# A hybrid decoder trunk: the written order kept on three engines during the channel MLPs, and the mixer's steps spread over each of them

## The chip, the cores and the metric

The kernel runs on one core of a Trainium2 chip. The metric is the device time of one execution in microseconds (us). Three runs of the kernel before took 2379.74, 2380.16 and 2384.47 us; their median, 2380.16 us, is the time to compare with. In what follows PE is TensorE, DVE is VectorE, ACT is ScalarE and SP is the engine whose queue issues the transfers; PEld rows are PE's weight loads.

## The reference, cut to what matters

Two layers over 1024 tokens of width 1024, in fp32:

```python
for i in range(DEPTH):                       # DEPTH = 2
    z = rmsnorm(h) @ w_in                    # 1024 -> 1280
    ya = chunk_gmlp(z_a)                     # gated MLP over chunks of 128 tokens
    yb = swa_sink_attention(z_q, z_k, z_v)   # 8 heads, window of 128 tokens, a sink per head
    yc = s5_ssm(z_c)                         # 16 groups of a complex recurrence, and a GLU
    h = h + concat(norm(ya), norm(yb), norm(yc)) @ w_out
    h = h + square(relu(norm(h) @ w_ff1)) @ w_ff2              # 1024 -> 4096 -> 1024
    h = h + sigmoid(norm(h) @ w_ple_gate) * (p[i] @ w_ple_proj)
```

The first four lines of the loop are called the mixer here, the last two the channel MLP and the gate.

## The kernel before

The tokens are cut into two halves of 512 columns. Every product is made of three matmuls in a split format (high x high, low x high, high x low), each 128 x 128 weights against 512 columns. So each weight tile is cast once on ACT (`load_w`, L104: the high part) and once on DVE (L105: the low part), and waits in a ring of three for the MLP (`ringf`) and of two for the mixer (`ringm`).

After a prelude (about 0 to 385 us: the mixer of layer 0 for half 0, projections of both halves) come four **windows**, one for each layer and half: (0,0), (0,1), (1,0), (1,1). In a window, `window()` writes eight chunks of the channel MLP and then eight gate tiles. A chunk has an up part, four tiles of 24 matmuls, each read by DVE (`r`, L1344), squared twice on ACT (`A`, `q`, L1346 and L1347) and split by DVE (L1348); and a down part, eight tiles of 12 matmuls, each added to `H` by DVE (L1333). In the last chunk each of these also feeds the sum of squares `nacc` and the next `x`. From `nacc` a matmul and a chain that changes between DVE and ACT (`rstd_wide`) make the scale `rbc`. A gate tile is 24 matmuls, then `gt` on DVE (L1390), a tanh on ACT (L1391), two operations on DVE (L1392, L1394, which finishes `H`), and in layer 1 four transposes on PE (`po`, L1400), a copy on ACT and the store. In layer 0 the window instead ends with `rstd_lane`, which makes the next layer's scale (`rv`, `dg`) and spreads it with a matmul.

While a window is written, the mixer of the half that comes next is written too, as a **lane**: a generator that yields after each step. After every 12 matmuls of the window `main` calls `tick`, and each lane advances by its rate:

```python
    def tick(self):
        for e in list(self.lanes):
            e[2] += e[1]
            while e[2] >= 1.0 and not e[3]:
                e[2] -= 1.0
                self.step(e)
```

In attention one step makes the scores `pss` of a unit (four heads of a block of 128 queries) and its softmax (`anm`, `pr`, `aden` on DVE, four exponentials on ACT), another its transposes `pt` and the product `po`, another the transposed queries `pq`.

None of this fixes the order on the engines. The code runs under a scheduler that sees the whole program, and places the instructions of each engine by its own forecast of when their inputs are ready; the order written serves as priority. Each engine then runs its list from front to end, as the rows of the trace do.

Of the kernel before, what the change touches and what calls it, by code (L numbers as in the profile page):

```python
# [38 lines left out]
PASSES = ((0, 0), (1, 0), (0, 1))  # L39


RATE, RATE0, RATEL = 3.0, 2.0, 3.0


class Ring:
# [11 lines left out]
    def next(self):  # L57
        while len(self.loaded) <= self.ahead and self.load():
            pass
        return self.loaded.pop(0)  # L60


class Trunk:
# [1033 lines left out]
    def k_steps(self, c):  # L1097


        V, S, T, at, nb, k = self.V, self.S, self.T, c["at"], c["nb"], c["k"]  # L1100
        fl = lambda x: x.rearrange("p h b a -> p (h b) a")
        f = fl(self.hf)[:, c["b0"]:c["b0"] + nb, 8:10]
        V.tensor_tensor(k, k, f.unsqueeze(3).to_broadcast([P, nb, 2, 64]), ALU.mult)
        t2 = at.tile([P, nb, 2, 64], F32, tag="rt2", name="kt2")
        tc, ts = c["tab"][1][:, 0], c["tab"][1][:, 1]
        for s in range(2):
            V.tensor_tensor(t2[:, :, :, s * 32:s * 32 + 32], k[:, :, :, 32 - s * 32:64 - s * 32],
                            ts[:, :, s].unsqueeze(2).to_broadcast([P, nb, 2, 32]), ALU.mult)
        V.tensor_tensor(k, k, tc.rearrange("p b a d -> p b (a d)").unsqueeze(2).to_broadcast([P, nb, 2, 64]), ALU.mult)
        V.tensor_tensor(k, k, t2, ALU.add)  # L1110
        c["kT"] = at.tile([P, 2, 2, nb, P], F32R, name="kT")
        yield
        for i in range(nb):
            kst = at.tile([P, 2, 3, 64], F32R, tag="kst", name="kst")
            S.copy(kst[:, :, 0], k[:, i])
            S.copy(kst[:, :, 2], k[:, i])
            V.tensor_tensor(kst[:, :, 1], k[:, i], kst.bitcast(F32)[:, :, 0], ALU.subtract)
            pk = self.ps.tile([P, 512], F32, tag="t", name="pk")
            for j in range(4):
                T.matmul(pk[:, j * P:(j + 1) * P], kst[:, j // 2, j % 2:j % 2 + 2].rearrange("p a d -> p (a d)"),  # L1120
                         self.identr, start=True, stop=True)
            S.copy(c["kT"][:, :, :, i], pk.rearrange("p (g s c) -> p g s c", g=2, s=2))
            yield
# [31 lines left out]
    def attn_steps(self, c, ql):  # L1155

        h = c["h"]
        units = [(4 * h + b, gk) for b in range(4) for gk in range(2)]
        n, st, late = len(units), {}, []
        for p in range(-1, n + 3):  # L1160
            if 0 <= p - 2 < n:
                blk, gk = units[p - 2]
                self.attn_pv(c, blk, gk, st.pop(p - 2))
                if gk == 1:
                    yield from self.wait(("z", c["l"], h))
                    self.attn_sum(c, blk)
                    if blk % 2:
                        late.append((p, blk - 1, self.attn_rstd(c)))
            if 0 <= p - 1 < n:
                self.attn_pt(c, *units[p - 1], st[p - 1])  # L1170
            yield
            if late and late[0][0] < p:
                self.attn_out(c, *late.pop(0)[1:])
            if 0 <= p < n:
                st[p] = self.attn_softmax(c, *units[p], self.attn_scores(c, *units[p], st[p]))
            yield
            if p + 1 < n:
                blk, gk = units[p + 1]
                st[p + 1] = self.attn_q(c, blk, gk)
                if gk:  # L1180
                    next(ql, None)
            yield

    def attn_q(self, c, blk, gk):
        qst = c["qst"][blk]
        pq = self.ps.tile([P, 512], F32, tag="t", name="pq")
        for i in range(4):
            self.T.matmul(pq[:, i * P:(i + 1) * P], qst[:, gk * 4 + i].rearrange("p a d -> p (a d)"), self.identr,
                          start=True, stop=True)
        qt = c["at"].tile([P, 4, P], F32R, name="qt")  # L1190
        self.S.copy(qt.rearrange("p a b -> p (a b)"), pq)
        return qt
# [286 lines left out]
    def run(self):  # L1479
        self.setup()  # L1480
        zws, self.zw = ExitStack(), None
        self.zw = self.pool(zws, "zw", 4, side=self.side(0), reuse_waits="tile")
        xs, xp = self.stage("xin", 0)
        left = self.lane(self.left_lane(), RATEL)
        for _ in self.first_x(0, xp, left):
            pass
        x1 = self.lane(self.first_x(1, xp))
        gen = self.project0()
        z0 = self.lane(gen)
        self.until(lambda: x1[3] and ("zq", 0, 0) in self.flags)  # L1490
        xs.close()
        self.until(lambda: {"zg", "rotary"} <= self.flags)
        zws.close()
        self.lanes.remove(z0)
        pzs = ExitStack()
        self.zpools.append(self.pool(pzs, "pz", 2, side=self.side(0), reuse_waits="tile"))
        self.lane(self.gmlp(0, 0, 0, "x", [("attn", 0, 0)]), RATE0)
        self.until(lambda: True)
        self.lane(self.attention(0, 0, 0), RATE0)
        self.main(gen)  # L1500
        self.main(self.embed())
        self.until(lambda: {("attn", 0, 0), ("gm", 0, 0)} <= self.flags)
        self.zpools.pop()
        pzs.close()
        self.finish(self.lane(self.mix_out(0, 0, self.fring, "mm", 3)))
        seq = [(l, h) for l in range(DEPTH) for h in range(2)]
        nxt = left
        for i, (l, h) in enumerate(seq):
            self.window(l, h, self.stages(*seq[i + 1]) if i + 1 < len(seq) else set())
            if i + 1 < len(seq):  # L1510
                self.finish(nxt)
            if i + 2 < len(seq):
                nxt = self.lane(self.mix_lane(*seq[i + 2]), RATE)


def build(tc, a):
# [27 lines left out]
```

## Time and profile before

| | |
|---|---|
| median of three runs | 2380.16 us |
| the profiled execution, its own time | 2385.95 us |
| its span, first to last instruction | 2384.2 us |
| PE busy, share of the span | 98% |
| PE weight loads busy | 79% |
| DVE busy | 65% |
| ACT busy | 43% |
| mean granted TensorE clock | 0.990 |
| chain that ended last: PE's share | 83% |

The profile is of one execution; 1.75 us of its time lie outside the span. Ends of matmuls are modelled, so PE counts as busy a little beyond the moment at which it could issue the next one. A row of the timeline gives the start, the duration and, in brackets, how long the engine was idle before it and what released it.

### The profile page before, as it was taken

What the parts mean: (1) busy time and instruction counts of PE and PEld (TensorE: products, weight loads), DVE (VectorE), ACT (ScalarE), POOL (GpSimd) and SP (SyncE); (2) the same over time, 40 slices, a digit from 0 to 9 for tenths busy, and PEclk for the clock granted to TensorE, in tenths of its full rate; (3) what the DMA queues carried; (4) which work ended last, traced back from release to release, by engine and by line L of the source; (5) the groups of instructions that cost most, each with busy time, mean ns of one, the idle gap of its engine ahead of it and who ended that gap; (6) DMA issues with size and microseconds to landing.
All of it is one profiled execution on the core that took longest, in us unless ns stands there. A gap on an engine that the chain in (4) does not pass through costs nothing.

```text
span 2384.2 us, 29265 instructions
## 1 busy us (share of the span) xinstructions
PE 2325.3 (98%) x10941; PEld 1885.4 (79%) x10941; DVE 1552.8 (65%) x2700; ACT 1027.8 (43%) x1787; POOL 5.4 (0%) x15
## 2 busy tenths in 40 slices
PE   7998899999999999999999999999999999999998
PEld 5886687788788887777888888777888887888887
DVE  7877767675966765676585774676657674444455
ACT  7427646433334443553342543464334343322333
POOL 0000000000000000000000000000000000000000
PEclk9998999999999999999999999999999999999999
DMA  8663632253553335324443344522534334333333
GB/s 244 188 203 119 208 99 64 80 173 106 145 156 102 111 125 155 95 78 140 123 135 124 98 145 124 145 72 76 166 105 135 124 97 134 97 96 94 94 97 98
DMA packets 403558, 295.94 MB, mean 124 GB/s; under 512 B 66668, under 2 KB 376024, under 8 KB 401624
## 3 DMA queue, kind: packets, MB, share of 16 engines
q1 hardware_dynamic: 403416, 294.07, 41.1%
q8 instruction: 86, 1.41, 0.3%
q14 instruction: 56, 0.46, 0.1%
HBM read 250.48 MB, written 43.54 MB: 123 GB/s over the span
## 4 chain that ended last, share of the span: by engine, by line
PE 83%; DMA 7%; DVE 5%; ACT 3%; issue 2%; SPq 1%; ACTq 0%; DVEq 0%
PE mm_ps L359 43%; PE x_ps L359 20%; PE s_ps L359 8%; DMA st<-in_w_in 2%; DVE w L105 2%; PE s_ps L710 1%; PE po L1259 1%; PE pss L1201 1%; ACT w L104 1%; PE p_ps L359 1%; DMA st<-in_w_out 1%; PE p_ps L947 1%; DMA yu<-ye 1%; PE pt L1238 1%; SPq L98 1%
## 5 line engine op out<-in xcount | busy, mean ns | idle before, releaser
L104 ACT CAST w<-st 128x1024 fp32r<-128x1024 f32 x364 | 387.9, 1067 | 853.1 <-PE mm_ps L359 430.0
L359 PE MATMUL mm_ps<-x,w 128*128 128x512 f32 x2904 | 708.4, 396 | 7.9 <-ACT x L89 4.2
L359 PEld LDWEIGHTS mm_ps<-x,w 128*128 128x128 f32 x2904 | 544.5, 190 | 133.0 <-issue 10.1
L105 DVE TENSOR_TENSOR w<-st,w 128x1024 fp32r<-128x1024 f32 x364 | 448.5, 1234 | 202.6 <-ACT w L104 191.6
L359 PE MATMUL mm_ps<-A,w 128*128 128x512 f32 x2016 | 500.8, 392 | 2.5 <-DVE H L1333 2.5
L359 PEld LDWEIGHTS mm_ps<-A,w 128*128 128x128 f32 x2016 | 375.7, 188 | 85.4 <-DVE H L1333 4.9
L359 PE MATMUL x_ps<-A,w 128*128 128x512 f32 x1056 | 272.8, 393 | 4.1 <-DVE H L1333 4.1
L359 PE MATMUL x_ps<-x,w 128*128 128x512 f32 x1104 | 272.2, 394 | 0.0
L359 PE MATMUL s_ps<-x,w 128*128 128x512 f32 x1056 | 252.4, 391 | 4.8 <-DVE w L105 2.6
L359 PEld LDWEIGHTS x_ps<-x,w 128*128 128x128 f32 x1104 | 205.6, 188 | 45.6 <-issue 3.4
L359 PEld LDWEIGHTS s_ps<-x,w 128*128 128x128 f32 x1056 | 198.1, 188 | 49.1 <-DVE w L105 4.0
L359 PEld LDWEIGHTS x_ps<-A,w 128*128 128x128 f32 x1056 | 196.5, 188 | 51.0 <-DVE H L1333 8.3
L1333 DVE TENSOR_TENSOR H<-H,mm_ps 128x512 f32<-128x512 f32 x168 | 113.2, 683 | 84.2 <-PE mm_ps L359 83.3
L1344 DVE SCALAR_TENSOR_TENSOR r<-mm_ps,rbc 128x512 f32<-128x512 f32 x88 | 60.7, 690 | 119.2 <-PE mm_ps L359 119.2
L710 PE MATMUL s_ps<-w,x 128*128 128x512 f32 x384 | 101.3, 404 | 4.1 <-ACT x L89 2.6
L1333 DVE TENSOR_TENSOR H<-H,x_ps 128x512 f32<-128x512 f32 x88 | 60.2, 684 | 68.8 <-PE x_ps L359 68.2
L1348 DVE TENSOR_TENSOR A<-q,A 128x512 fp32r<-128x512 f32 x128 | 87.8, 686 | 6.8 <-ACT q L1347 6.6
L710 PEld LDWEIGHTS s_ps<-w,x 128*128 128x128 f32 x384 | 73.6, 194 | 20.8 <-ACT x L89 3.0
L1346 ACT ACTIVATE A<-r 128x512 fp32r<-128x512 f32 x128 | 80.2, 627 | 8.1 <-DVE r L1344 7.9
L1347 ACT ACTIVATE q<-r 128x512 f32<-128x512 f32 x128 | 78.9, 617 | 0.0
L1224 ACT ACTIVATE pr<-pr,anm,hf 128x128 f32<-128x128 f32 x128 | 61.6, 485 | 17.4 <-DVE anm L1221 17.4
L89 ACT ACTIVATE x<-H,gT 128x512 fp32r<-128x512 f32 x80 | 53.7, 711 | 13.5 <-PE s_ps L359 7.7
(386 smaller groups left out, 2112.3 us busy)
## 6 DMA issues: line engine op xcount, KB each, us to landing
st<-in_w_ff SPq DMA_DIRECT2D x256, 512.0 KB, 4.1
st<-in_w_out SPq DMA_DIRECT2D x32, 512.0 KB, 4.1
st<-in_w_ple_gate SPq DMA_DIRECT2D x32, 512.0 KB, 4.1
st<-in_w_in SPq DMA_DIRECT2D x18, 512.0 KB, 4.4
p<-par SPq DMA_DIRECT2D x8, 1024.0 KB, 8.5
pj<-pjz SPq DMA_DIRECT2D x32, 256.0 KB, 2.2
H<-hs SPq DMA_DIRECT2D x4, 2048.0 KB, 7.9
pj<-pj SPq DMA_DIRECT2D x32, 256.0 KB, 3.4
```

The costliest lines, as they stand in the source:

```text
L89: self.S.activation(hi, x, AF.Copy, scale=g)
L98: self.Q.dma_start(sv[:, :, c0:c1], src)
L104: self.S.copy(hi, src)
L105: self.V.tensor_tensor(lo, src, hi.bitcast(F32), ALU.subtract)
L359: self.T.matmul(ps, w[:, i, k, c0:c0 + P], X[:, j, k, :], start=(start and n == 0), stop=(stop and n == last))
L710: T.matmul(pss[b], X[:, j, 2 * s + kk, c], w[:, i, kk, :], start=(s == 0 and kk == 0 and n == 0), stop=(s == 3 and kk == 1 and n == 2))
L1224: S.activation(pr[:, i], pr[:, i], AF.Exp, bias=nm[:, i:i + 1], scale=f[:, i:i + 1], accum_out=den[:, i:i + 1])
L1333: V.tensor_tensor(H[:, m], H[:, m], ps, ALU.add)
L1344: V.scalar_tensor_tensor(r, ps, 0.0, self.R[h][1], ALU.max, ALU.mult)
L1346: S.activation(A[:, 0, m], r, AF.Square)
L1347: S.activation(q, r, AF.Square)
L1348: V.tensor_tensor(A[:, 1, m], q, A.bitcast(F32)[:, 0, m], ALU.subtract)
```

## The change

Three things change. All four windows are written inside `manual_schedule` for PE, DVE and ACT: on these three engines the instructions of that part keep the order in which the code writes them. SP's and POOL's order stays the scheduler's. The rate of a mixer lane falls from 3.0 steps a tick to 1.15, and that of the lane that runs on into the first window to 1.25. And two yields are added, one in `k_steps` and one in each round of `attn_steps`, except in the prelude's attention: a round is four steps long where it was three.

```diff
-RATE, RATE0, RATEL = 3.0, 2.0, 3.0
+RATE, RATEW, RATE0, RATEL = 1.15, 1.25, 2.0, 3.0
+ENGINES = {mybir.EngineType.PE, mybir.EngineType.DVE, mybir.EngineType.Activation}
@@ k_steps
         c["kT"] = at.tile([P, 2, 2, nb, P], F32R, name="kT")
         yield
+        if c["l"] or c["h"]:
+            yield
@@ attn_steps
             yield
+            if c["l"] or h:
+                yield
@@ run
         nxt = left
-        for i, (l, h) in enumerate(seq):
-            self.window(l, h, self.stages(*seq[i + 1]) if i + 1 < len(seq) else set())
-            if i + 1 < len(seq):
-                self.finish(nxt)
-            if i + 2 < len(seq):
-                nxt = self.lane(self.mix_lane(*seq[i + 2]), RATE)
+        nxt[1] = RATEW
+        with self.tc.manual_schedule(engines=ENGINES):
+            for i, (l, h) in enumerate(seq):
+                self.window(l, h, self.stages(*seq[i + 1]) if i + 1 < len(seq) else set())
+                if i + 1 < len(seq):
+                    self.finish(nxt)
+                if i + 2 < len(seq):
+                    nxt = self.lane(self.mix_lane(*seq[i + 2]), RATE)
```

The work is the same. What moves is the order on each engine, at three places above all. (The lines of the change stand 4 to 11 lower than those of before: L359 becomes L363, L1400 becomes L1408.)

First, PE at the very end, in the gate tiles of the last window. `s_ps`, `p_ps`, `x_ps` and `mm_ps` are the gate tiles, `po` the transposes of a finished `H`. Before:

```order
L359 MATMUL mm_ps<-x_18296,w 128x512 x24
L359 MATMUL s_ps<-x_18296,w 128x512 x24
L359 MATMUL p_ps<-x_18296,w 128x512 x24
L359 MATMUL mm_ps<-x_18296,w 128x512 x4
L1400 MATMUL po<-identr,H_13998 128x128 x4
L359 MATMUL mm_ps<-x_18296,w 128x512 x20
L359 MATMUL s_ps<-x_18296,w 128x512 x2
L1400 MATMUL po<-identr,H_13998 128x128 x4
```

And now, from the last rows of the down part on:

```order
L292 MATMUL o_ps<-nacc,onesr 128x512
L363 MATMUL s_ps<-x_18298,w 128x512 x24
L1408 MATMUL po<-identr,H_15295 128x128 x4
L363 MATMUL x_ps<-x_18298,w 128x512 x24
L1408 MATMUL po<-identr,H_15295 128x128 x4
L363 MATMUL mm_ps<-x_18298,w 128x512 x24
L1408 MATMUL po<-identr,H_15295 128x128 x4
```

The first transposes stood behind five gate tiles and four matmuls of the sixth; now those of each tile stand directly behind its own 24 matmuls.

Second, PE at the end of the first window, where the next layer's scale is made (`o_ps<-onesr,nacc` sums the squares, `o_ps<-dg,onesr` spreads the scale; `w,x_7513` and `w,x_7515` are the next mixer's projection). Before:

```order
L359 MATMUL mm_ps<-x_5521,w 128x512 x9
L273 MATMUL o_ps<-onesr,nacc 128x1 x4
L359 MATMUL mm_ps<-x_5521,w 128x512 x15
L359 MATMUL x_ps<-x_5521,w 128x512 x20
L317 MATMUL o_ps<-dg,onesr 128x512
L359 MATMUL x_ps<-x_5521,w 128x512 x4
```

Now:

```order
L363 MATMUL s_ps<-x_6990,w 128x512 x24
L363 MATMUL x_ps<-x_6990,w 128x512 x24
L277 MATMUL o_ps<-onesr,nacc 128x1 x4
L321 MATMUL o_ps<-dg,onesr 128x512 x2
L363 MATMUL mm_ps<-x_6627,w 128x512 x12
L714 MATMUL s_ps<-w,x_7515 128x512 x12
```

The 35 matmuls of the next window that stood between the two, and the 9 and more before the first, now follow both.

Third, DVE in the attention of the first window. Before, one softmax in the down part of a chunk:

```order
L1214 COPY_PREDICATED pr<-pmask,pss 128x256 x2
L1219 TENSOR_REDUCE anm<-pr 128x4
L1220 TENSOR_TENSOR anm<-anm,nhf 128x4
L1221 TENSOR_TENSOR anm<-anm,nsk 128x4
L1227 TENSOR_TENSOR aes<-anm,sinks 128x4
L1333 TENSOR_TENSOR H_3113<-H_3113,x_ps 128x512
L1333 TENSOR_TENSOR H_3113<-H_3113,mm_ps 128x512 x2
L1229 TENSOR_TENSOR aden<-aden,aes 128x4
L1230 RECIPROCAL aden<-aden 128x4
L1231 TENSOR_TENSOR pr<-pr,aden 128x512
```

Now, one in the up part:

```order
L1222 COPY_PREDICATED pr<-pmask,pss 128x256 x2
L1227 TENSOR_REDUCE anm<-pr 128x4
L1228 TENSOR_TENSOR anm<-anm,nhf 128x4
L1229 TENSOR_TENSOR anm<-anm,nsk 128x4
L1235 TENSOR_TENSOR aes<-anm,sinks 128x4
L1237 TENSOR_TENSOR aden<-aden,aes 128x4
L1238 RECIPROCAL aden<-aden 128x4
L1239 TENSOR_TENSOR pr<-pr,aden 128x512
L1352 SCALAR_TENSOR_TENSOR r<-mm_ps,rbc 128x512
L1356 TENSOR_TENSOR A<-q,A 128x512
L109 TENSOR_TENSOR w<-st,w 128x1024
```

Nothing of the window stands any more between `aes`, whose exponentials ACT makes, and `aden`, which needs them; the tile's `r` and, directly behind it, the `A` that needs ACT's `q`, follow the whole softmax.

## Rows read from the trace of the kernel before

**Rows 1.** The page: busy us, share of the span, instructions.

```profile
PE 2325.3 (98%) x10941; PEld 1885.4 (79%) x10941; DVE 1552.8 (65%) x2700; ACT 1027.8 (43%) x1787; POOL 5.4 (0%) x15
```

**Rows 2.** Stretches, one per window: length, busy PE, PEld, DVE, ACT, POOL; clock, DMA.

```profile
385.00:860.00 475.00, 473.52 (x2252) 382.79 (x2251) 336.74 (x545) 201.47 (x325) 0.95 (x1) 1.00 0.41 123
860.00:1428.00 568.00, 561.83 (x2641) 456.34 (x2640) 373.99 (x607) 245.99 (x414) 0.96 (x1) 1.00 0.40 119
1428.00:1990.00 562.00, 555.65 (x2634) 450.82 (x2633) 361.69 (x584) 237.00 (x400) 0.95 (x1) 1.00 0.39 117
1990.00:2375.00 385.00, 381.84 (x1676) 312.86 (x1675) 191.73 (x238) 121.16 (x161) 0.00 (x0) 1.00 0.33 98
```

**Rows 3.** Timeline of PE in the last window: start, us, instructions.

```profile
2101.62 2.88 PE L359 MATMUL x_ps<-A,w 128*128 128x512 f32 x12
2104.34 2.88 PE L359 MATMUL mm_ps<-A,w 128*128 128x512 f32 x12
```

**Rows 4.** Timeline: the last gate tile, and the last copy before the end.

```profile
2373.55 0.71 PE L359 MATMUL x_ps<-x,w 128*128 128x512 f32 x2
...
2374.30 0.69 DVE L1390 TENSOR_TENSOR gt<-x_ps,rbc 128x512 f32<-128x512 f32 x1 [3.33 <-PE x_ps L359]
...
2376.41 0.69 DVE L1394 SCALAR_TENSOR_TENSOR H<-gt,H 128x512 f32<-128x512 f32 x1
...
2380.45 0.59 ACT L1402 COPY ot<-po 128x512 f32<-128x512 f32 x1 [1.25 <-PE po L1400]
```

**Rows 5.** Timeline: the chain of `rstd_wide` ahead of the last gate tiles.

```profile
2337.92 0.70 DVE L289 TENSOR_SCALAR o_ps<-o_ps 128x512 f32<-128x512 f32 x1 [5.00 <-PE o_ps L288]
...
2338.65 0.69 DVE L293 TENSOR_SCALAR rbc<-o_ps 128x512 int32<-128x512 int32 x1
...
2343.06 0.63 ACT L295 ACTIVATE rs_a<-rbc 128x512 f32<-128x512 f32 x1 [2.05 <-DVE rbc L297]
...
2344.45 0.69 DVE L297 SCALAR_TENSOR_TENSOR rbc<-rs_a,rbc 128x512 f32<-128x512 f32 x1
```

**Rows 6.** Timeline: from the last `H` of the first window to `dg`.

```profile
851.09 0.69 DVE L1394 SCALAR_TENSOR_TENSOR H<-gt,H 128x512 f32<-128x512 f32 x1
...
852.54 0.69 DVE L329 TENSOR_TENSOR nacc<-nacc,nsq 128x512 f32<-128x512 f32 x1 [0.76 <-ACT nsq L328]
...
859.05 0.16 DVE L275 TENSOR_SCALAR rv<-o_ps 128x4 f32<-128x4 f32 x1 [1.27 <-PE o_ps L273]
...
861.48 0.68 DVE L310 TENSOR_TENSOR dg<-identr,rtm 128x512 fp32r<-128x512 f32 x1
```

**Rows 7.** Timeline: one softmax that DVE met with nothing else to do.

```profile
436.55 0.85 ACT L1212 COPY pr<-pss 128x256 f32<-128x256 f32 x2 [0.41 <-PE pss L1201]
...
436.95 0.93 DVE L1214 COPY_PREDICATED pr<-pmask,pss 128x256 f32<-128x256 int32 x2
...
441.18 0.16 DVE L1229 TENSOR_TENSOR aden<-aden,aes 128x4 f32<-128x4 f32 x1 [1.99 <-ACT aes L1228]
```

**Rows 8.** Timeline: DVE's three operations for one tile of the up part.

```profile
434.03 0.69 DVE L1344 SCALAR_TENSOR_TENSOR r<-mm_ps,rbc 128x512 f32<-128x512 f32 x1 [1.60 <-PE mm_ps L359]
...
435.12 1.23 DVE L105 TENSOR_TENSOR w<-st,w 128x1024 fp32r<-128x1024 f32 x1 [0.40 <-ACT w L104]
...
436.26 0.69 DVE L1348 TENSOR_TENSOR A<-q,A 128x512 fp32r<-128x512 f32 x1
```

**Rows 9.** Stretches around two waits of PE; columns as in rows 2.

```profile
962.00:965.00 3.00, 0.80 (x5) 0.38 (x4) 1.74 (x3) 2.82 (x5) 0.00 (x0) 1.00 0.03 11
965.00:968.50 3.50, 3.50 (x12) 2.83 (x12) 2.35 (x4) 1.74 (x5) 0.00 (x0) 0.52 0.65 188
...
931.00:933.40 2.40, 0.99 (x6) 0.49 (x4) 2.02 (x2) 2.40 (x5) 0.00 (x0) 1.00 0.56 200
933.40:938.00 4.60, 4.60 (x21) 3.81 (x22) 4.19 (x16) 0.25 (x1) 0.00 (x0) 1.00 0.74 177
```

## The prediction

> **What bounds the kernel now.** I read the page first: PE is busy for 98% of the span, DVE for 65%, ACT for 43% [rows 1]. So the question is only what keeps PE's matmuls from following one another. The stretches of the four windows come next. PE is idle for 475 - 473.52 = 1.48 us in the first, 6.17 and 6.35 in the two after it and 3.16 in the last, 17.2 us in all, at a clock of 1.00 [rows 2]. Busy time includes modelled ends, so I checked it by counting. In the timeline twelve matmuls of 512 columns take 2104.34 - 2101.62 = 2.72 us, 0.227 each [rows 3]. The last window's 1676 instructions at that pace are 380.4 of its 385 us, a loss of 4.6 where the idle time says 3.2; by that ratio all four windows lose about 25 us. That is all that a better order of the same matmuls can bring, and a worse order can lose much more: the other engines' chains are hidden today only because the scheduler put ready matmuls beside them.
>
> The Trainium skill says in "Perfetto Trace Analysis", section "Identifying the Most-Contended Engine", that matmul busy time tells badly how near a kernel is to its limit, and that the busy share of LDWEIGHTS tells better. By its figure here, about 80%, there would be more room than 25 us; the trace bears it out only where other matmuls than the steady ones run. The row's own bound: weight loads take 312.86/1675 = 0.187 us each in the last window [rows 2], 82.4% of a 0.227 us interval, against 80.6, 80.3, 80.2 and 81.3% in the four windows. If all windows came up to 82.4% they would gain 10 + 15 + 15 + 5 = 45 us. I take 25 (term G), bounds 17 and 45.
>
> **The change part by part.** The instructions stay the same; the price is in what PE finds at the head of its list, since it runs its list from front to end.
>
> *A, the gate tiles of layer 1.* Each tile's four transposes now follow its own 24 matmuls directly, and they need the finished `H`. In the last gate tile of before, PE starts the last pair of matmuls at 2373.55 and could start the next at 2374.0; `gt` starts at 2374.30, and `H` ends at 2376.41 + 0.69 = 2377.10 [rows 4]. Nothing behind the transposes can pass them, so PE waits 3.1 us in each tile. Three tiles differ. The first of the last window must also see `rstd_wide` finish on DVE: 2337.92 to 2345.14, 7.2 us [rows 5]; with one low part `w` of 1.23 [rows 8] and the gate's chain of 2.8, less its own matmuls of 24 x 0.227 = 5.4, about 6. In the third window lane matmuls stand behind the same chain, so its first tile costs about 3, but eight splits of the next `x` (8 x 0.69) are ahead of its second tile's `gt` on DVE: 7.2 + 5.5 + 2.8 - 2.7 = 13. Twelve ordinary tiles are 37, with 6 + 3 + 13 it is 59. The end gets shorter: from 2374.0 to 2384.2 it is 10.2 us today, with two groups of transposes; a chain of 3.1 + 0.6 + 0.6 (copy) + 3.2 (store, from 2381.04 to the end) is 7.5. A = 59 - 3 = **+56**. Nothing can cover this but the order itself; I see no lower bound under 50.
>
> *B, the ends of the windows.* After the down part the sum `o_ps<-nacc` now follows the last matmul: `H` 0.69, square and add 853.23 - 851.78 = 1.45 [rows 6], and 0.3 from engine to engine: 2.4 in each of four windows, 10, and I add 4 for DVE being late with the tail's longer list. At the two ends of layer 0 the sum follows the last gate tile (2.8 + 1.45 + 0.3 = 4.6), and the spreading of the scale follows the sum at once: `rv` to the end of `dg` is 859.05 to 862.16, 3.1 us [rows 6], a second `dg` 0.7, hops 0.4. That is 8.7 each, 17 for two. Before, 35 matmuls lay between. B = **+31**, bounds 25 and 35.
>
> *C, attention in the windows.* Now DVE executes the whole softmax before the window's next `r`, and waits in it for ACT's exponentials: one softmax runs from 436.95 to `aden` at 441.18, of which 1.99 is waiting [rows 7]; with the reciprocal and the last product it holds DVE for 5.3. The unit's other work there I count as five operations of 0.69, 3.5: 8.8. A window's up tile takes DVE 2.23 from `r` to the start of `A`, 0.69 for `A` and 1.23 for a `w`, 4.1 [rows 8]; that the wait inside it is no longer filled is new too. Two tiles of a down part take 2 x 0.69 + 1.23 = 2.6. The mean for 24 matmuls is 3.4. A round has four steps; at 1.25 steps a tick it is spread over 4/1.25 x 12 = 38 matmuls of the window, at 1.15 over 42. DVE then needs 8.8 + 38/24 x 3.4 = 14.2 us a unit, and 14.7. PE needs 38 x 0.227 + 2.5 = 11.2, and 12.0. (The 2.5 is chosen: the first window has 1728 long matmuls of its own, 392 of 475 us, and I give each of eight units 2.5 of the 83 that are left.) So PE waits 3.0 us a unit in the first window and 2.7 in the next two: 8 x 3.0 + 16 x 2.7 = **+67**. Bounds: if DVE's wait for ACT counts for nothing, 8 x 1.0 + 16 x 0.7 = 19; if each softmax delays PE by its whole 5.3, 24 x 5.3 = 127. I take the balance of DVE against PE, since it is made of measured durations and PSUM banks can only move a lasting deficit.
>
> *D, the lane's own chains.* The other scales of the mixer (nine chains like rows 5) and the steps for `k` now stand in order on DVE. Their consumers on PE come later by at least a tick of 2.7 us, and free banks cover most of the rest: **+10**, bounds 0 and 40.
>
> *Clock.* After PE had idled 3.00 - 0.80 = 2.2 us, the granted clock was 0.52 in the next 3.5 us; after 1.4 us of idle it stayed at 1.00 [rows 9]. At half clock (1.2 of 2.4 GHz) 3.5 us lose 0.48 x 3.5 = 1.7. A, B and the longest waits of C make some 24 idle times of over 2.2 us. I let half of them cost 1.7: **+20**, bounds 0 and 60. The Trainium skill warns in "TensorE: Matmul & The Clock Gate", section "HAM oscillation — how this bites in real kernels", that short bursts of matmuls between repeated waits run at the low clock again and again; by that rule every one of these 24 would pay, 40 instead of 20, and the one wait of rows 9 that is long enough agrees with it.
>
> The two yields and the lower rates issue nothing by themselves. PE changes less often between the window's and the lane's matmuls; what that may bring is within G.
>
> Sum: 56 + 31 + 67 + 10 + 20 - 25 = +159, on the profiled execution's 2385.95 us: 2545. The median of the runs is 5.8 lower than that execution: **2539 us**.
>
> **The rivals.**
>
> *Only the fixed waits cost.* PE's lead through its PSUM banks, and the lower rate of the lane, carry attention over: C at 19, D at 0, clock at 10. 56 + 31 + 19 + 10 - 25 = +91, **2471 us**. For it speaks that DVE is busy for only 65% [rows 1]; against it, that the balance in C is negative in every unit, and a lead is spent after one or two.
>
> *Attention is worse.* Each softmax delays `r`, so that `A` and the down part are late as well, and the clock falls at most waits: C at 127, D at 20, clock at 40: +249, **2629 us**. For it: `r` to `A` has become a wait of 2.2 us that nothing fills. Against it: PE has several banks free when a softmax begins.
>
> *Faster.* The weight loads are the true bound, and an order in which PE's stretches are longer brings PE to 82.4%: -45 in the windows, **2335 us**, if the transposes find `H` ready. It decides against this rival that they can't: 16 of them with 3.1 us each are more than the whole 45. It would need a window loss before of over 90 us, where I count 25.
>
> *No effect.* The order written is nearly what the engines execute today, and the waits only move: 2380 us. The moved transposes speak against it.
>
> **How the numbers follow.** The forecast gets 0.60, with 2490 to 2595 as its own range (C between 40 and 100, clock between 0 and 40); the fixed waits alone 0.19, attention worse 0.15, faster 0.04, no effect 0.02. A range from 2450 to 2640 takes in the first three but for some 0.12 at their edges. This kernel's measurement can tell about 0.2% from no change; of the cases only the last lies within that, so faster 0.04, same 0.02, slower 0.94.
>
> **What the changed profile would show.** For A: idle time of some 3.1 us ahead of each group of `po` transposes, released by DVE's `H`, about 50 us in all, and DVE idle with it. For B: two waits of 8 to 9 us ahead of the sums `o_ps` at the ends of the two layer-0 windows, and four of 2.4. For C: waits of PE for DVE's `r` and `H` (a bank not yet read) in the first half or so of three windows, and DVE idle ahead of `aden` for 2 us in nearly each of 24 softmaxes. For the clock: tenths of 7 or 8 in the slices of gates and attention. PE's busy share should fall to about 92%. The last window has no lane, so its 385 us show A alone: about 420 with the clock.
>
> The prediction is wrong if DVE keeps ahead of PE in attention in spite of the softmax (C near 0), if a wait of PE does not bring the clock down (or brings it down for much longer than 3.5 us), or if the windows before hid more loss than I count.

## The result, and the profile of the changed kernel

The changed kernel takes 2797.39 us (median of four runs, 2794.89 to 2802.74); the kernel before, in the same comparison, 2380.98 us. The ratio is 1.1749, with a 95% interval from 1.1728 to 1.1771: slower by 416 us, where the forecast was 159 us and its range ended at 2640.

The page of the profiled execution (2802.74 us, of which 2801.0 are its span): busy time by engine, then PE's granted clock in 40 slices, here and before.

```profile
PE 2454.2 (88%) x10941; PEld 1967.7 (70%) x10941; DVE 1600.9 (57%) x2700; ACT 1030.5 (37%) x1787; POOL 5.4 (0%) x15
...
PEclk9989989997899899999989989999998988999997
```

```profile
PEclk9998999999999999999999999999999999999999
```

Against [rows 1] the instructions are the same in number. PE's busy time has grown by 2454.2 - 2325.3 = 129 us, and its idle time from 2384.2 - 2325.3 = 59 us to 2801.0 - 2454.2 = 347 us, by 288. The two add up to the 417 us by which the span is longer. The growth of the busy time is the clock's: by the trace's clock records PE is busy for 296 us at half clock, before for 39, and half of the difference is 129. The slices show it too: eleven of them stand at 7 or 8 tenths, from the third to the last, where one did before, and the mean clock of the execution is 0.927 instead of 0.990. So the loss has two parts, waits of 288 us and a clock of 129 us. Up to 330 us both executions lie on one another (the same run of matmuls starts at 329.67 before and at 329.71 after); all of the loss comes later.

Stretches of the changed kernel, cut by what the lane does (columns as in [rows 2]). There are 19; the rows are attention of the first window, its gated MLP with the tables prepared beside it, the window's end, the projection of the second lane, the gates of the third window, the last window without a lane, its end and gates, and the sum over all 19:

```profile
330.00:532.00 202.00, 167.00 (x770) 130.74 (x769) 126.31 (x234) 89.32 (x201) 0.96 (x1) 0.92 0.21 64
...
650.00:750.00 100.00, 69.09 (x286) 51.65 (x287) 71.28 (x131) 28.77 (x42) 0.00 (x0) 0.81 0.37 112
...
890.00:985.00 95.00, 75.46 (x311) 60.66 (x310) 64.39 (x97) 41.77 (x60) 0.00 (x0) 0.90 0.35 106
985.00:1110.00 125.00, 125.00 (x550) 103.46 (x549) 53.71 (x71) 38.36 (x49) 0.00 (x0) 0.99 0.44 129
...
2250.00:2350.00 100.00, 65.29 (x236) 50.74 (x236) 42.25 (x57) 26.89 (x39) 0.00 (x0) 0.80 0.25 72
2350.00:2700.00 350.00, 348.33 (x1531) 287.66 (x1530) 170.86 (x200) 106.56 (x139) 0.00 (x0) 1.00 0.33 99
2700.00:2801.00 101.00, 64.36 (x226) 49.57 (x226) 34.62 (x46) 20.06 (x30) 0.00 (x0) 0.79 0.20 57
sum 2471.00, PE 2155.99 PEld 1728.37 DVE 1366.68 ACT 849.25 POOL 2.86; mean PE 113.47 PEld 90.97 DVE 71.93 ACT 44.70 POOL 0.15
```

The kernel before, from 330 us on:

```profile
330.00:2384.00 2054.00, 2027.17 (x9455) 1646.65 (x9453) 1304.77 (x2046) 841.50 (x1380) 2.86 (x3) 1.00 0.38 114
```

PE idles for 2471 - 2156 = 315 us in all, against 2054 - 2027 = 27 us before. By stage, as length less busy time of each stretch: attention with the steps of `k` 35.0, 29.3 and 29.3 in its three windows; gated MLP 30.9, 19.4 and 16.5; state-space part 14.2, 5.6 and 11.5; the lane's output 6.9, 4.6 and 1.3; the two ends of layer 0 19.5 and 17.9; the gates of layer 1 34.7 and 36.6. The projections, which feed PE with matmuls of their own, lose nothing, and the 350 us of the last window without a lane lose 1.7. Where PE idles long the clock is low too: 0.78 to 0.81 in the gates and the gated MLP, 0.99 or 1.00 where nothing waits.

Who waited for whom, PE's list from 330 us on (us in total, how often, the longest):

```profile
PE po L1408 <- DVE H L1402: 55.0, 15, 13.2
PE mm_ps L363 <- ACT A L1354: 28.0, 10, 5.3
PE x_ps L363 <- ACT A L1354: 26.0, 7, 8.6
PE pk L1126 <- DVE kst L1123: 24.9, 8, 12.2
PE o_ps L292 <- DVE nacc L333: 22.7, 7, 8.0
PE o_ps L277 <- DVE nacc L333: 18.0, 2, 9.9
PE mm_ps L363 <- DVE H L1341: 17.4, 6, 6.2
PE t_ps L292 <- DVE os L1281: 15.6, 6, 5.4
```

Before, the largest sum and the longest wait of the same list were:

```profile
PE po L1400 <- ACT ot L1402: 4.7, 6, 1.0
...
PE pk L1120 <- DVE kst L1117: 3.4, 2, 2.2
```

The places of the forecast are there: `po` behind `H`, `o_ps` behind `nacc`, `A` and `H` of the window's tiles. `pk` (the transposed keys) and `t_ps` (a sum of squares of the lane), which were to share the 10 us of term D, wait 40.5 us by themselves.

### The profile page after: what moved, and what is told of

Its sections match the earlier page's. It is cut to its first block, busy times and chain, and to the rows that moved or that the text cites. A ratio compares the mean times of both kernels' runs of the same rounds, so it can differ in the third digit from the quotient of the medians.

```text
span 2801.0 us, 29236 instructions
## 1 busy us (share of the span) xinstructions
PE 2454.2 (88%) x10941; PEld 1967.7 (70%) x10941; DVE 1600.9 (57%) x2700; ACT 1030.5 (37%) x1787; POOL 5.4 (0%) x15
## 4 chain that ended last, share of the span: by engine, by line
PE 34%; DVE 11%; ACT 6%; issue 3%; DMA 1%; SPq 0%; ACTq 0%; DVEq 0%
PE mm_ps L363 17%; PE x_ps L363 9%; PE s_ps L363 3%; ACT w L108 2%; DVE w L109 2%; DVE x L94 1%; PE s_ps L714 1%; DVE H L1341 1%; ACT x L93 1%; DVE rs_a L300 1%; DVE gt L1400 1%; DVE H L1402 1%; DVE gt L1398 1%; DVE rbc L301 1%; ACT rs_a L299 1%
## 5 line engine op out<-in xcount | busy, mean ns | idle before, releaser
L363 PE MATMUL mm_ps<-x,w 128*128 128x512 f32 x2904 | 722.3, 404 | 13.6 <-ACT x L93 8.1
L363 PEld LDWEIGHTS mm_ps<-x,w 128*128 128x128 f32 x2904 | 558.6, 194 | 143.2 <-ACT x L93 9.3
L363 PE MATMUL mm_ps<-A,w 128*128 128x512 f32 x2016 | 522.6, 411 | 47.9 <-ACT A L1354 28.0
L363 PEld LDWEIGHTS mm_ps<-A,w 128*128 128x128 f32 x2016 | 396.1, 199 | 146.9 <-ACT A L1354 32.5
L363 PE MATMUL x_ps<-A,w 128*128 128x512 f32 x1056 | 280.5, 412 | 41.6 <-ACT A L1354 26.0
L363 PE MATMUL s_ps<-x,w 128*128 128x512 f32 x1056 | 269.0, 408 | 14.0 <-ACT x L93 13.9
L363 PEld LDWEIGHTS x_ps<-A,w 128*128 128x128 f32 x1056 | 207.5, 199 | 93.0 <-ACT A L1354 28.9
L363 PE MATMUL x_ps<-x,w 128*128 128x512 f32 x1104 | 269.3, 398 | 0.0
L363 PEld LDWEIGHTS s_ps<-x,w 128*128 128x128 f32 x1056 | 207.8, 198 | 64.1 <-ACT x L93 15.9
L363 PEld LDWEIGHTS x_ps<-x,w 128*128 128x128 f32 x1104 | 211.1, 193 | 45.1 <-issue 0.5
L332 ACT ACTIVATE nsq<-H 128x512 f32<-128x512 f32 x70 | 44.2, 631 | 149.1 <-DVE H L1318 79.5
```

The source lines that it names most:

```text
L332: self.S.activation(s, H[:, k], AF.Square)
L363: self.T.matmul(ps, w[:, i, k, c0:c0 + P], X[:, j, k, :], start=(start and n == 0), stop=(stop and n == last))
```

## The experiments

All runs are compared with runs of the kernel before on the same chip, whose medians were 2381 to 2384 us. A kernel whose edit says nothing else is the changed kernel with that edit.

| run | median us | ratio to before, 95% |
|---|---|---|
| the change | 2797.39 | 1.1749 (1.1728 to 1.1771) |
| rates_alone | 2377.41 | 0.9978 (0.9964 to 0.9991) |
| order_alone | 3007.04 | 1.2625 (1.2597 to 1.2654) |
| pe_only | 2634.60 | 1.1054 (1.1037 to 1.1070) |
| dve_only | 2778.11 | 1.1661 (1.1641 to 1.1681) |
| act_only | 2640.64 | 1.1081 (1.1061 to 1.1101) |
| dve_act_only | 2789.86 | 1.1707 (1.1690 to 1.1725) |
| po_later | 2728.29 | 1.1451 (1.1426 to 1.1477) |
| po_filled | 2769.16 | 1.1632 (1.1603 to 1.1660) |
| last_only | 2421.80 | 1.0167 (1.0147 to 1.0187) |
| gmlp_slow | 2755.95 | 1.1563 (1.1546 to 1.1580) |
| evac_first | 2802.93 | 1.1758 (1.1738 to 1.1777) |
| attn_slow | 2805.26 | 1.1773 (1.1755 to 1.1791) |
| attn_split | 2784.12 | 1.1690 (1.1661 to 1.1718) |
| up_ticks | 2795.16 | 1.1731 (1.1711 to 1.1751) |
| fine_attn | 2794.17 | 1.1738 (1.1719 to 1.1756) |
| paced_all | 2712.14 | 1.1382 (1.1360 to 1.1404) |
| fine_all | 2662.61 | 1.1184 (1.1159 to 1.1208) |
| paced_sched | 2435.15 | 1.0218 (1.0199 to 1.0237) |

### Is it the order or the rates?

rates_alone keeps the rates and yields and drops the fixed order (an empty `ExitStack` leaves it to the scheduler); order_alone the reverse.

```diff
# rates_alone
-        with self.tc.manual_schedule(engines=ENGINES):
+        with ExitStack():
# order_alone
-RATE, RATEW, RATE0, RATEL = 1.15, 1.25, 2.0, 3.0
+RATE, RATEW, RATE0, RATEL = 3.0, 3.0, 2.0, 3.0
@@ the two yields of the change are taken out
```

> The rates and the two yields of the change, with every engine's order left to the scheduler as before. Theory (the kept order makes the waits, and the waits make the clock fall): the scheduler moves the instructions as before, so 2381 us, at most 20 us either way. Rival (a lane spread over the whole window is what costs: its work comes too late): most of the 416 us, above 2600 us.

> The kept order on the three engines with the old rates of 3.0 and without the two yields. Theory: the same kinds of waits, with more of the lane's work ahead of each of the window's operations on VectorE, so at least the 2797 us of the change, about 2850. Rival (the spreading costs): near 2450 us, with only the gates' and the window ends' waits.

The order costs all of it. With the scheduler's order the rates make no loss, and even a gain of 0.2% (interval 0.09 to 0.36%): rates_alone is the one version here that is faster than both kernels, than the one before by 5 to 7 us. In a fixed order the old rates, without the two yields, are worse by 210 us than the new ones, more than the 50 us expected: the change's spreading is a remedy, not the harm.

### The gates: a wait and what it does to the clock

po_later writes the transposes of a tile behind the matmuls of the next one; po_filled puts matmuls whose product nothing reads into the wait.

```diff
# po_later, in the gate loop of layer 1 (put() holds the old lines)
-                po = self.ps.tile([P, 4, P], F32, tag="t", name="po")
...
+                done.append(m)
+                if m:
+                    put(done.pop(0))
# po_filled
+                for b in range(12):
+                    T.matmul(po.rearrange("p a b -> p (a b)"), self.identr, self.X[h][:, 0, 0, :],
+                             start=True, stop=True)
                 for b in range(4):
                     T.transpose(po[:, b], H[:, m, b * P:(b + 1) * P], self.ident)
```

> The change, but in layer 1 the transposes of a gate tile are written behind the 24 matmuls of the next tile. Leaves nothing out. Theory (each of these waits costs its 3 us and then about 1.7 us of half clock): some 50 us of waits and 25 us of clock come back, 2797 - 75 = 2722 us, and the clock in the last gates is 1.00. Rival (the half clock has another cause than these waits): only the waits come back, about 2747 us, with the clock still near 0.8 there.

> The change, with twelve matmuls of 128x512 that nothing reads put ahead of each group of transposes in layer 1: 2.7 us of work inside a wait of 3.1 us. The result is the same. Theory (the idle time is what brings the clock down): the wait stays, but the clock stays at 1.00 and some 15 x 1.7 = 25 us come back, about 2770 us. Rival (the clock falls for another cause): 2797 us or a few more, with the clock still at about 0.8 in the gates.

First the timeline of one gate tile in the changed kernel and a stretch of its last gates, then, for po_filled, a stretch of the last gates of the same length and one tile of them, then a tile of po_later:

```profile
2740.81 0.69 DVE L1402 SCALAR_TENSOR_TENSOR H<-gt,H 128x512 f32<-128x512 f32 x1
...
2741.65 1.08 PE L1408 MATMUL po<-identr,H 128*128 128x128 f32 x4 [2.99 <-DVE H L1402]
...
2752.05 1.08 PE L1408 MATMUL po<-identr,H 128*128 128x128 f32 x4 [2.99 <-DVE H L1402]
```

```profile
2731.00:2796.00 65.00, 47.00 (x168) 36.83 (x168) 17.36 (x22) 11.06 (x16) 0.00 (x0) 0.82 0.19 53
```

```profile
2693.00:2758.00 65.00, 61.88 (x272) 48.77 (x271) 21.22 (x27) 13.26 (x19) 0.00 (x0) 0.97 0.27 77
```

```profile
2716.18 0.66 PE L1411 MATMUL po<-identr,H 128*128 128x128 f32 x4
2716.59 5.74 PE L363 MATMUL s_ps<-x,w 128*128 128x512 f32 x24
2722.17 2.96 PE L1408 MATMUL po<-x,identr 128*128 128x512 f32 x12
2725.24 0.66 PE L1411 MATMUL po<-identr,H 128*128 128x128 f32 x4
```

```profile
2683.73 5.75 PE L363 MATMUL mm_ps<-x,w 128*128 128x512 f32 x24
2689.32 0.60 PE L1399 MATMUL po<-identr,H 128*128 128x128 f32 x4
2689.68 5.74 PE L363 MATMUL s_ps<-x,w 128*128 128x512 f32 x24
```

In the changed kernel `H` ends at 2741.50, the transposes start 0.15 later after a wait of 2.99 us, and the 24 matmuls of the next tile follow them. The next group of transposes starts at 2752.05, so a tile takes 10.40 us. In po_filled, where PE works for that time, the chain is just as long (2722.17 to 2725.24), but a tile takes 2725.24 - 2716.18 = 9.06 us, and the clock in this stretch is 0.97 instead of 0.82. In po_later a tile takes 2689.68 - 2683.73 = 5.95 us, which is its matmuls and transposes. Both runs came out within 7 us of what was expected. po_filled shows that PE's idle time itself brings the clock down there: with the same chain and 192 matmuls more it is faster by 28 us.

last_only keeps the order in the last window alone:

```diff
-        with self.tc.manual_schedule(engines=ENGINES):
-            for i, (l, h) in enumerate(seq):
+        for i, (l, h) in enumerate(seq):
+            with ExitStack() if i < 3 else self.tc.manual_schedule(engines=ENGINES):
```

> The change's rates and yields, with the written order kept in the last window alone, where there is no lane. Theory (the terms A and B add to the rest): on 2377 us of the rates alone come one wait of 8 us, eight waits of 3.1 us and about 14 us of clock, less 3 us at the end: 2377 + 44 = 2421 us. Rival (part of them was already lost before, or the scheduler places the earlier windows worse beside a fixed end): 2400 us, or above 2440 us.

```profile
2330.00:2424.00 94.00, 65.06 (x226) 50.33 (x224) 29.31 (x38) 17.26 (x25) 0.00 (x0) 0.79 0.20 56
```

2421.80 us: the terms of the last window add, and it has them complete (29 us idle in the last 94, clock 0.79). In this window, which has no lane, the fixed order costs 44 us, most of it at the window's end.

### Which engine's order?

```diff
# pe_only, dve_only, act_only, dve_act_only: one or two of the three
-ENGINES = {mybir.EngineType.PE, mybir.EngineType.DVE, mybir.EngineType.Activation}
+ENGINES = {mybir.EngineType.DVE}
```

> The change, with the written order kept on TensorE alone; VectorE's and ScalarE's order is the scheduler's. Theory (TensorE's order makes the waits at the gates and the window ends, about 106 us with some 45 of clock; VectorE's and ScalarE's order makes those of attention and the gated MLP): about 2560 us. Rival (TensorE's order makes nearly all of it, whatever the others do): above 2700 us.

> The change, with the written order kept on VectorE and ScalarE alone. Theory: TensorE can put other matmuls beside the gates' and window ends' chains, but what VectorE has not read keeps the banks, so part of the waits of attention and of the gated MLP stays: about 2500 us. Rival (only TensorE's order costs): 2385 us.

> The change, with the written order kept on VectorE alone. Theory (it is VectorE's list, with the mixer's steps ahead of r, H and the low parts of the weights, that holds TensorE up): about 2650 us. Rival (the weights' casts in ScalarE's list are what the run with both lists kept waits for): below 2480 us.

> The change, with the written order kept on ScalarE alone. By the theory of VectorE's list: about 2500 us, since each cast of a weight stands behind the tanh or the exponentials of what was written before it. By the rival (ScalarE's list and its casts): about 2700 us.

PE's two largest waits in dve_only, then the largest in act_only:

```profile
PE mm_ps L363 <- DVE r L1352: 66.1, 14, 11.8
PE mm_ps L363 <- DVE w L109: 49.1, 16, 14.2
```

```profile
PE mm_ps L363 <- ACT w L108: 47.8, 17, 12.9
```

The parts don't add: TensorE's list costs 251 us alone, VectorE's 394, ScalarE's 257, and the three together 416. Each run was slower than its theory said: pe_only by 75 us, dve_only by 128, act_only by 141, dve_act_only by 290. One fixed list is enough to cost 250 us. VectorE's alone makes 95% of the loss, and leaving PE free beside VectorE and ScalarE (dve_act_only) saves only 7 us of the change, where 300 were expected. When PE is free it waits for other things instead. The largest sum in dve_only, 66.1 us, is for `r`, which reads the bank that PE wants to write next; no such wait stands in the list of the change. The next is for weights. In the written order the cast of a weight tile (ScalarE) and its low part (VectorE) stand behind the tanh, the copies and the lane's steps written before them: 49.1 us of waits for low parts at `mm_ps` alone in dve_only, 47.8 us for casts in act_only. In the kernel before no wait for a cast or a low part came to more than 2.6 us in all.

### The lane's stages

gmlp_slow gives the gated MLP more ticks.

```diff
+    def slow(self, gen, n):
+        for i, _ in enumerate(gen):
+            yield
+            if i % n == 0:
+                yield
...
-        yield from self.gmlp(l, h, h)
+        yield from self.slow(self.gmlp(l, h, h), 2)
@@ left_lane: the same with n = 1 around both(prep, gmlp)
```

> The change, with more ticks for the gated MLP of the mixer: in the first window two ticks for each step of it (and of the tables prepared beside it), in the two others three ticks for two steps. These stretches lose 78 us of waits and 32 of clock in the change. Theory (too much work of VectorE for the matmuls that lie beside it): about half comes back, 2797 - 50 = 2747 us. Rival (the waits are chains inside one step, which a slower lane doesn't shorten): 2797 us, at most 15 less.

The gated MLP's three stretches (the sum over them, cut closer than above), in the change and in gmlp_slow:

```profile
sum 208.00, PE 152.66 PEld 115.89 DVE 145.45 ACT 56.99 POOL 0.00; mean PE 50.89 PEld 38.63 DVE 48.48 ACT 19.00 POOL 0.00
```

```profile
sum 243.00, PE 204.64 PEld 161.88 DVE 173.14 ACT 77.03 POOL 0.00; mean PE 68.21 PEld 53.96 DVE 57.71 ACT 25.68 POOL 0.00
```

Idle falls from 55.3 us to 38.4, and the clock recovers (0.83, 0.79 and 0.86 become 0.94, 0.93 and 0.95); 41 us come back in all, near the 50 expected. How such a wait is made, in the timeline of the change:

```profile
1440.14 1.22 DVE L1003 TENSOR_REDUCE lmu<-vg 128x16 f32<-128x1024 f32 x1
...
1441.60 1.22 DVE L1006 TENSOR_TENSOR vg<-vg,lmu 128x1024 f32<-128x1024 f32 x1
1442.74 0.68 DVE L1352 SCALAR_TENSOR_TENSOR r<-mm_ps,rbc 128x512 f32<-128x512 f32 x1
...
1444.14 2.04 PE L363 MATMUL mm_ps<-A,w 128*128 128x512 f32 x3 [3.12 <-ACT A L1354]
```

VectorE has the lane's operations in its list, 1440.14 to 1442.74, before it may read PE's finished tile at 1442.74; ScalarE squares it, and PE's down part goes on at 1444.14 after 3.12 us of waiting. Two of the lane's operations take 1.22 us each, for 1024 columns.

Five kernels ask what makes attention wait. evac_first moves the tick behind the tile's own operations; attn_slow spreads a unit over 64 matmuls of the window instead of 42, and hurries projection and output; up_ticks takes the lane's steps away from the last two tiles of an up part; attn_split moves the sum that waits for the exponentials into a later step, and fine_attn cuts the steps of attention to what was estimated as 2.5 us of VectorE at most.

```diff
# evac_first: main(gen, hold) leaves out the last tick; it comes behind r, A, q, A or H
+                self.tick()
# attn_slow: a rate for each stage (projection, attention, ssm, gated MLP, output)
+PACE = (2.5, 0.75, 1.15, 1.15, 1.8)
+PACE0 = (0.8, 1.25, 1.25, 1.8)
# up_ticks
-                self.main(self.cm(ps, w, 0, self.X[h], range(NK)))
+                self.main(self.cm(ps, w, 0, self.X[h], range(NK)), 2 if m < 2 else 0)
# attn_split and fine_attn: aden and pr in the next step
+            if 0 <= p < n:
+                self.attn_scale(st[p])
# fine_attn also: a yield inside q_steps, in each round of the root, and after each split of attn_out
```

> The change, but the tick after a tile's last matmuls comes behind the tile's own r, A, q or H, so that a step of the lane no longer stands ahead of them on VectorE and ScalarE. Theory 1 (it is the place in VectorE's list that makes TensorE wait for A and H, 84 us in all): about half of that and of its clock comes back, 2797 - 65 = 2730 us. Theory 2 (VectorE has more to do there than TensorE, as the balance of the prediction has it, wherever it stands): within 20 us of 2797.

> The change, with a pace for each stage of the lane in place of one rate: attention 0.75 steps a tick (0.8 in the first window), projection 2.5, the mixer's output 1.8, the rest as in the change. A unit of attention then lies over 64 matmuls of the window instead of 42 (60 instead of 38). Theory (the balance of the prediction: VectorE 8.8 us a unit plus 3.4 for 24 matmuls, TensorE 0.227 a matmul plus 2.5): a deficit of 0.9 us a unit instead of 2.7, so of the 93 us that these stretches lose with their clock some 60 come back: 2737 us. Rival (each softmax delays TensorE by a fixed amount, however far apart they stand): 2797 us, or more, since projection and output are faster.

> The change, but in an up part the lane's four ticks of the third and fourth tile are given in the first and second, so that no step of the lane stands in VectorE's and ScalarE's lists behind the start of the third tile until the down part has begun. Theory (TensorE has no reserve where a down part needs the A of the last up tile, so any step of the lane there is a wait): TensorE's waits for A, 54 us, and some 20 us of clock go, and about as much as a third comes back as waits elsewhere: 2797 - 50 = 2747 us. Rival (VectorE is late by the same sum wherever the steps stand): within 15 us of 2797.

> The change, with a softmax cut in two: the sum, the reciprocal and the product with it (aden, pr) come a step later, in the step of the queries, so that VectorE doesn't wait 2 us for the exponentials in the middle of its list. Theory (what a step costs TensorE is how long VectorE is held in it): about a third of the 107 us that the three stretches of attention lose with their clock comes back, 2797 - 35 = 2762 us. Rival (the waits come from elsewhere, such as the steps of q and the low parts): within 10 us of 2797.

> The change, with the steps of attention cut finer over the same number of ticks (75 steps in 46 ticks in place of 55 in 47): the softmax in two, the steps of q in two, the sum of squares, its root (three rounds of it) and the output's splits each in steps of their own. The spread and the work are the same; the longest hold of VectorE by one step falls from some 9 us to about 2.5. Theory (a step costs TensorE what it holds VectorE beyond TensorE's reserve of a tile or less): about half of the 118 us that attention loses with its clock comes back, 2797 - 50 = 2747 us. Rival (the lists move in lock step, and the waits go to whatever stands next, as in up_ticks): within 15 us of 2797.

The three stretches of attention as a sum, first in the change, then in attn_slow, then in fine_attn:

```profile
sum 574.00, PE 481.59 PEld 377.46 DVE 342.96 ACT 239.68 POOL 2.86; mean PE 160.53 PEld 125.82 DVE 114.32 ACT 79.89 POOL 0.95
```

```profile
sum 760.00, PE 679.54 PEld 537.27 DVE 435.42 ACT 293.85 POOL 2.87; mean PE 226.51 PEld 179.09 DVE 145.14 ACT 97.95 POOL 0.96
```

```profile
sum 537.00, PE 452.93 PEld 357.94 DVE 332.45 ACT 233.90 POOL 2.86; mean PE 150.98 PEld 119.31 DVE 110.82 ACT 77.97 POOL 0.95
```

Idle is 574 - 481.6 = 92.4 us in the change, 80.5 in attn_slow and 84.1 in fine_attn. The balance of the prediction wanted a third of the deficit in attn_slow (0.9 us a unit instead of 2.7); it is not the cause. (The time of attn_slow says less: outside these stretches, with projection and output hurried, PE idles for 29 us more than in the change.) Nor is the place in the tile (evac_first, whose interval overlaps the change's) or in the chunk. In up_ticks the 54 us of waits for `A` all but vanish from the list, but the kernel took as long, and others grew:

```profile
PE pt L1247 <- DVE pr L1240: 23.6, 9, 6.0
...
PE mm_ps L364 <- ACT w L108: 12.5, 3, 8.0
```

`pt` was 10.1 us in the change, and the only wait of a window's tile for a cast above 2 us was one of 4.0. With finer steps, too, others grew as the waits for `A` and `H` shrank: `pt` in attention, and outside it, at the windows' ends and in the lane's output, `o_ps`, which was 22.7 us:

```profile
PE o_ps L294 <- DVE nacc L335: 49.3, 8, 16.5
...
PE pt L1264 <- DVE pr L1257: 31.9, 10, 6.1
```

The exponentials are not settled. VectorE's waits for them from 330 us on, in the change and in attn_split:

```profile
DVE aden L1237 <- ACT aes L1236: 47.7, 24, 2.0
```

```profile
DVE aden L1244 <- ACT aes L1238: 24.8, 14, 2.0
```

attn_split took away only half of them, and the kernel became 13 us faster, where 35 were expected. What all of them cost PE was not measured.

paced_all and fine_all put the remedies together (paces for all stages, po_later; fine_all with the fine steps too and a less hurried projection).

> The change, with attention and the gated MLP both slower in the way of attn_slow and gmlp_slow, projection and output faster, and the transposes of layer 1 a tile later as in po_later. Theory (the losses are separate and add up): 2797 - 69 - 41 - 60 = 2627 us. Rival (the waits only move to the next stage, which finds its banks late): above 2680 us.

> fine_attn with a slower gated MLP (0.9 and 0.75 steps a tick), somewhat faster projection and output (1.6 and 1.5) and the transposes of layer 1 a tile later. Theory (finer steps, a slower gated MLP and the moved transposes add up): 2797 - 50 - 35 - 69 = 2643 us. Rival (only the moved transposes and the gated MLP count): about 2695 us.

Both fell short, by 85 and by 20 us. fine_all, the best kernel here with all three lists fixed throughout, gives back 135 of 416 us. po_later alone gave 69; if that adds, 66 belong to the rest, where 85 were expected. Its paces are not paced_all's, so what the fine steps do in it isn't known apart. paced_sched shows that a pace isn't free under the scheduler either:

> The scheduler's order on every engine, with the paces of paced_all for the lane (attention 0.78 steps a tick, gated MLP 0.75, projection 2.5, output 2.0). Theory (the scheduler hides what the pace leaves): within 10 us of the 2377 us of the rates alone. Rival (a lane that is more even serves the scheduler better too): 2365 us or less.

It is slower by 2.2%, so under the scheduler the even rate of rates_alone is better than a slow attention between a fast projection and a fast output. Which of the paces costs it was not tried.

## Why the prediction was wrong

The direction, and the kind of mechanism, were right: PE waits in order for chains that the scheduler had covered. By its terms:

- **A, 56 us: right.** 55.0 us of waits of `po` for `H`: one of 13.2, where 13 was forecast, and 14 that make 41.8, or 3.0 each, where 3.1 was. The first group of the last window waits 5.5 more (6 forecast) by a releaser that the profile doesn't name. last_only came out as worked out from these. (Before, four groups of transposes stood behind the last matmuls, not two as the prediction read; its 10.2 us to the end hold all the same.)
- **B, 31 us: too small.** Of the 22.7 us for `nacc` 20.6 stand behind the four down parts (the rest is the lane's); with the 18.0 at the ends of layer 0 and the 6.7 for `dg` they are 45. The forecast took 2.4 us for the wait after a down part; it is 8.0 in the first and the last window, 3.3 and 1.3 in the two where the lane's matmuls lie beside it. At the ends of layer 0 it took 4.6 for the sum, which waits 8.1 and 9.9. The 4 us allowed for VectorE's longer list in the tail were not worked out; VectorE's rows for a tile there, in the last window:

```profile
2700.35 1.22 DVE L109 TENSOR_TENSOR w<-st,w 128x1024 fp32r<-128x1024 f32 x1 [0.18 <-ACT w L108]
2701.49 0.68 DVE L1341 TENSOR_TENSOR H<-H,x_ps 128x512 f32<-128x512 f32 x1
2702.93 0.69 DVE L333 TENSOR_TENSOR nacc<-nacc,nsq 128x512 f32<-128x512 f32 x1 [0.76 <-ACT nsq L332]
2703.54 0.75 DVE L94 SCALAR_TENSOR_TENSOR x<-H,gT,x 128x512 fp32r<-128x512 f32 x1
2704.21 0.68 DVE L1341 TENSOR_TENSOR H<-H,mm_ps 128x512 f32<-128x512 f32 x1
```

  `H`, a wait of 0.76 for ScalarE, `nacc` and the split of `x` are 2.72 us a tile, and every second tile a low part of 1.22 and its wait of 0.18 come on top: 3.4 us where PE takes 12 x 0.227 = 2.72. Over eight tiles VectorE falls 5.4 us behind, and 5.4 + 2.4 is nearly the 8.0.
- **C, 67 us: near in size, the reason wrong.** Attention idles 92.4 us; without the 24.9 of `pk` and the 15.6 of `t_ps`, which belong to D, 52 are left. But the balance of VectorE against TensorE does not hold: in attn_slow, where it wanted a third, 43 are left (80.5 - 21.6 - 15.6). So it is an accident that 67 is near. VectorE's idle time ahead of `aden` came as forecast, 2 us in each of 24 softmaxes.
- **D, 10 us, bounds 0 and 40: the step that failed most.** "Their consumers on PE come later by at least a tick of 2.7 us, and free banks cover most of the rest" is what the runs contradict. The steps of `k` wait 24.9 us, the scales of attention (`t_ps`) 15.6, the gated MLP's stretches idle 67 us, the state-space part's 31 and the output's 13: 151 us in place of 10. The consumers to look at were not only the lane's own matmuls but the window's tiles, whose `r` and `H` stand in VectorE's list behind the lane's steps, as in the timeline of the gated MLP. The forecast looked for that in attention only.
- **Clock, 20 us, bounds 0 and 60: the other step that failed, 129 us.** It was mis-sized twice over. First, there are not 24 long waits: counted from the starts of PE's matmuls, 62 waits after 330 us are over 2 us (one before). Second, nearly every one pays: in 54 of the 62 a stretch at half clock begins during the wait or within 1.5 us of its end. The trace's clock records have 61 such stretches in the whole execution, against 9 before. So a long wait costs 129/62 = 2.1 us of clock on the average, where half of 1.7 was allowed [rows 9]. The rule of the Trainium skill that stood against the forecast ("TensorE: Matmul & The Clock Gate", section "HAM oscillation — how this bites in real kernels") tells of a kernel in which, after each of its repeated waits of some 3 to 5 us, the matmuls start at the low clock again. This trace agrees for 54 of 62 waits, the gates' 2.99 us among them. Of the ten shorter than 3 us, counted from the starts, four paid, so the prediction stretched the page where it let it speak for all of its 24, counted from 2.2 us up.
- **G, -25 us: right, as bookkeeping.** The 27 us of idle time before are the part of the 315 that was there already. That a better order could win them is not shown: rates_alone, the fastest version, gains 5 to 7 us.

With what was measured the sum nearly closes: 60 + 45 + 52 + 151 + 129 - 27 = 410, of 417. Of the 258 us that the forecast missed, 141 are D, 109 are clock and 14 are B; C was 15 too large.

What stays open is why attention's own waits move and hardly shrink. Shown is that VectorE's list alone is enough for 95% of the loss, that the three lists' losses don't add, and that in up_ticks and fine_attn waits grew elsewhere as those of one place went. Which quantity limits a round of attention was not found: VectorE's work per matmul, and the place or the length of a step, do not explain it, and the wait for the exponentials was only half taken away.

## What to carry to other kernels

When a scheduler's order is replaced by a written one, list every chain between engines that is issued beside the bound engine's work, not only the ones that the diff touches, and price each by what stands ahead of its consumer in the list of the engine in the middle. Here the fixed list of an engine of 65% load was enough for 95% of the loss, in a kernel whose bound engine had been busy for 98%. Price a long wait of TensorE with what it does to the clock too: here 2 us more on the average of 62 waits, and 1.3 for the gates' waits of 3 us.

## What was not expected of the hardware

Work that nobody reads can make a kernel faster. In the last gates TensorE's clock had a mean of 0.82 beside waits of 3 us; with the waits filled by matmuls that nothing reads it was 0.97, and the kernel took 28 us less though the chains stayed as long. Beside a wait of 2.99 us this is 1.3 us a tile (10.40 to 9.06).
